# Splitting layer 0's output weights in small pieces behind the projections, and loading them ready-made

## The chip, the core and the metric

The kernel runs on one core of a Trainium2 chip. Its engines are TensorE (PE, with its weight loads shown as PEld), VectorE (DVE), ScalarE (ACT) and GpSimd (POOL). SyncE (SP) issues nearly all of the DMAs, one after the other in its own queue. The metric is the time of one execution on the device, in microseconds. Each engine works through its own instructions strictly in order, and waits at the first one whose operands or buffers are not ready.

## The reference

A two-layer encoder over 1024 tokens of width 1024, with 256 memory tokens. Layer 0 projects the normalised input to three groups of heads and a gate: A (windowed attention with a bias and a sink), B (dense attention) and X (attention into the memory). Layer 1 has differential attention in place of A and B. What matters here is the end of each layer:

```python
def even_layer(x, mem_n, ...):
    h = rmsnorm(x, norm_g)
    aq, ak, av, bq, bk, bv, xq, gate = _split(h @ w_in, EVEN_SPLITS)
    ...
    y = jnp.concatenate([y_a, y_b, y_x], axis=-1) * jax.nn.silu(gate)
    return x + y @ w_out        # y: 1024 x 1024, w_out: 1024 x 1024
```

## The kernel before

Every product of the projections is made from two parts of each operand: hi, the value rounded to the type in which TensorE multiplies (fp32r), and lo, the difference. One product is three matmuls (hi·hi, hi·lo, lo·hi). So every weight that is loaded has to be split first: a cast gives hi, a subtraction gives lo.

In layer 0 the projections are *jobs*, in the order of the table JORD (`xq0 m0 g6 m1 m2 g7 m3 bk bq0 bv bq1 g3 bq2 ak av aq0 g0 aq1 g4 g1 aq2 g5 g2`: q, k, v of the heads, m0 to m3 for the memory, g0 to g7 for the gate). A job yields after each *portion* of eight matmuls (`proj_jobs`), and the attention steps pull a few portions at a time (`Jobs.pull`), so that projection matmuls stand between the matmuls of attention. When the jobs run out, at about 380 us, parts of the output projection (`pre_jobs`, tiles `pre`) take their place, until `out_proj` does the rest (tiles `po`).

An attention step makes scores (`sb`, `sa`), a softmax on ACT, DVE and POOL (`e`, `mn`, `rz`), sends the result to a second tile by a DMA (`er<-e`, a "hop"), transposes it on TensorE (`te`, `ta`), splits it (`PTh` or `PTa` on ACT, `PTl` on DVE) and multiplies it with the values (`ob`, `oa`). `ab` is the bias band of an A head, which comes from `skew_d` in DRAM. `gy` is the gated result, `yr` and `xh` are later reads.

The output weights `w_out` of layer 0 are split in `load_wout`: 16 chunks of 128 × 512, each loaded raw (`wor`), cast on ACT (`woh`), and subtracted on DVE or POOL in turn (`wol`). This can begin only when the first half of the last job (g2) has freed the tiles of the layer's input, which `wout_hook` waits for. Layer 1's weights are split in another way: the class `Early` does it in 32 pieces of 128 × 256 during the attention, keeps hi and lo in DRAM (`wo_d`), and `load_wout` loads them ready-made.

The order of the instructions on each engine is set by the framework's list scheduler, from the order in which the program is written, its dependences and hints (`tc.issue_after`). `after_fill()` is such a hint: the instruction comes after the last matmul of the projections. The weights of the projections are loaded in two halves per job by `load_w` (tile `wr`, two buffers), cast on DVE (`wh`) and subtracted on POOL, or for the jobs m0 to m3 on DVE (`wl`).

Of the kernel before, what the change touches and what calls it, by code (L numbers as in the profile page):

```python
# [155 lines left out]
def encoder_kernel(ctx, tc, A):  # L156
# [15 lines left out]
    def dma(out, in_, eng=None):  # L172
        if out.dtype == F32R and in_.dtype == F32R:
            out, in_ = out.bitcast(F32), in_.bitcast(F32)
        (eng or nc.sync).dma_start(out=out, in_=in_)  # L175
# [20 lines left out]
    for t in (spare, edge):  # L196
# [50 lines left out]


    class Early:
        def __init__(self, l, tiles):  # L250
            self.l, self.n, self.tiles, self.held = l, 0, tiles, None
# [8 lines left out]
        def step(self):  # L260
            self.store()
            if self.n < 32:
                i, c = divmod(self.n, 2)
                nh, k = divmod(i, 8)
                c = c * 256
                self.n += 1
                raw = wp.tile([P, 512], F32, tag="wr", name="wor", bufs=2)[:, 0:256]
                dma(raw, w_out[self.l][KORD[self.l][k], :, nh * 512 + c:nh * 512 + c + 256])
                hi, lo = self.tiles()
                nc.scalar.copy(hi, raw)  # L270
                nc.gpsimd.tensor_tensor(out=lo, in0=raw, in1=hi, op=ALU.subtract)
# [6 lines left out]
    def load_wout(l, i, pl):  # L278
        nh, k = divmod(i, 8)
        if k == 0:  # L280
            wtile.append([pl.tile([P, 8, 512], F32R, tag="h", name="wo" + c, bufs=4) for c in "hl"])
        hi, lo = (t[:, k, :] for t in wtile[nh])
        if l == 1:
            for t, d in zip((hi, lo), wo_d[l][nh]):
                dma(t, d[:, k, :])
            return hi, lo
        raw = sg(M, "wor", F32) if i % 2 else wp.tile([P, 512], F32, tag="wr", name="wor", bufs=2)
        dma(raw, w_out[l][KORD[l][k], :, nh * 512:(nh + 1) * 512])
        nc.scalar.copy(hi, raw)
        (nc.gpsimd if i % 2 else nc.vector).tensor_tensor(out=lo, in0=raw, in1=hi, op=ALU.subtract)  # L290
        return hi, lo

    def wout_hook(l, jobs, last, pl):
# [104 lines left out]
    def sg(M, name="sg", dt=F32R):  # L398
        return M.pl.tile([P, 512], dt, tag="sg", name=name, bufs=M.cfg["sg"])
# [311 lines left out]
    def pre_jobs(l, src):  # L711
        out = []
        for ts, k in PRE[l]:
            parts = [(0,), (1,)] if len(ts) > 1 else [(0, 1)]
            for nhs in parts:
                out.append(dict(
                    tag="pre%s%d" % (ts[0], nhs[0]), also=tuple("pre%d" % t for t in ts) if nhs[-1] else (),
                    run=lambda _, ts=ts, k=k, nhs=nhs: pre_run(l, ts, k, nhs, src), load=lambda: None,
                    when=lambda k=k, nhs=nhs: len(wout) >= 8 * nhs[-1] + 8 and all((l, m) in stored for m in range(k))))
        return out  # L720

    def pre_run(l, ts, kn, nhs, src):
# [725 lines left out]

    toeps = {}

    def halves():
        t = sg(M, "wos")
        return t[:, 0:256], t[:, 256:512]
# [202 lines left out]
```

## Time and profile before

| | us |
|---|---|
| three runs | 1240.26, 1238.16, 1237.77 |
| their median | 1238.16 |
| the profiled execution | 1240.08 |
| its span in the profile | 1238.3 |
| PE busy | 1201.8 |
| DVE busy | 793.6 |
| ACT busy | 653.7 |
| POOL busy | 429.0 |

The span runs from the first to the last recorded instruction; the profiled execution's time has 1.8 us around it. In rows of the timeline stand the start, the duration, the engine, the line, the operation, what is written and read, the shape and the count; a bracket at the end tells how long the engine was idle before it and what ended that. In rows by tile, the three numbers are the shortest, median and longest duration in ns. In rows of DMA issues, the last number is the median time in us from issue to landing. In rows of windows, the busy time of each engine stands with its number of instructions, then the clock granted to TensorE, the DMA share and GB/s. The line numbers are those of the kernel before.

### The profile page before, as it was taken

Reading aid. Unit: us, or ns where it says so; the run is one execution under the profiler, and the core shown is the slowest. Engines: PE = TensorE matmul, PEld = TensorE weight load, DVE = VectorE, ACT = ScalarE, POOL = GpSimd, SP = SyncE. Lnnn points to the kernel's source line nnn. Section 1 sums busy time; section 2 is a strip of 40 time slices with the busy share of each in tenths; the row PEclk is TensorE's granted clock in tenths of the full one; section 3 lists DMA queues with packets and bytes.
Section 4 is the critical chain, followed back from the end, with each engine's and each line's share of the span. In section 5 each row is a group of like instructions: output and inputs, shape, how many; then the busy total and the mean of one; then the engine's idle time right before and its main releaser. Section 6 shows DMA issues by size and latency. Waiting matters only on the chain.

```text
span 1238.3 us, 19903 instructions
## 1 busy us (share of the span) xinstructions
PE 1201.8 (97%) x6806; PEld 1001.2 (81%) x6806; DVE 793.6 (64%) x1471; ACT 653.7 (53%) x1469; POOL 429.0 (35%) x414
## 2 busy tenths in 40 slices
PE   6999999999999899999999999999999999999997
PEld 5788888888887778887888778788887878888886
DVE  5547665477777768637355865766666666767544
ACT  6248754367667767533157744555545454445332
POOL 5023365466666655403122222334242231201100
PEclk9999999999999989999999999999999999999999
DMA  6654445545465565466644445354453452458353
GB/s 255 199 191 146 161 170 167 167 156 203 176 229 201 195 220 197 151 200 215 191 166 147 143 154 156 136 166 156 142 175 136 149 173 95 153 205 293 124 195 145
DMA packets 112769, 216.71 MB, mean 175 GB/s; under 512 B 13303, under 2 KB 45303, under 8 KB 112669
## 3 DMA queue, kind: packets, MB, share of 16 engines
q1 hardware_dynamic: 112668, 215.45, 51.7%
q8 instruction: 54, 0.88, 0.3%
q14 instruction: 47, 0.38, 0.1%
HBM read 87.71 MB, written 39.86 MB: 103 GB/s over the span
## 4 chain that ended last, share of the span: by engine, by line
PE 51%; DVE 1%; issue 1%; DMA 0%; SPq 0%; POOL 0%; ACT 0%; POOLq 0%; DVEq 0%; ACTq 0%
PE acc L329 26%; PE oc L1530 6%; PE po L695 5%; PE sc L1491 4%; PE te L573 3%; PE sc L1497 3%; PE pre L695 2%; PE ox L649 1%; PE ssqc L1545 1%; PE tv L438 1%; PE sx L542 1%; PE rbcc L1558 0%; PE tx L377 0%; DMA wr<-in_w_mem 0%; SPq L175 0%
## 5 line engine op out<-in xcount | busy, mean ns | idle before, releaser
L329 PE MATMUL acc<-h,wh 128*128 128x512 f32 x1536 | 499.5, 399 | 1.9 <-DVE h L351 0.8
L329 PEld LDWEIGHTS acc<-h,wh 128*128 128x128 f32 x1536 | 282.6, 188 | 66.4 <-issue 12.3
L329 PE MATMUL acc<-h,wl 128*128 128x512 f32 x768 | 304.5, 396 | 1.6 <-POOL wl L243 1.6
L243 POOL TENSOR_TENSOR wl<-wr,wh 128x512 fp32r<-128x512 f32 x96 | 125.1, 1304 | 303.5 <-DVE wh L241 132.0
L348 DVE TENSOR_TENSOR PTl<-te,PTh 128x512 fp32r<-128x512 f32 x224 | 148.3, 686 | 125.3 <-ACT PTh L347 122.7
L1506 ACT ACTIVATE e<-e,mn 128x1024 f32<-128x1024 f32 x96 | 110.1, 1148 | 123.7 <-DVE mn L1503 123.7
L329 PEld LDWEIGHTS acc<-h,wl 128*128 128x128 f32 x768 | 144.6, 188 | 35.3 <-issue 4.7
L347 ACT CAST PTh<-te 128x512 fp32r<-128x512 f32 x224 | 125.1, 591 | 18.7 <-PE te L573 15.4
L1503 DVE CUSTOM_DVE_ANT_0 e<-sc,toep 128x1024 f32<-128x1024 f32 x96 | 113.9, 1217 | 7.9 <-PE sc L1497 7.8
L1107 POOL TENSOR_TENSOR e<-e,rz 128x1024 f32<-128x1024 f32 x48 | 92.4, 1929 | 76.2 <-DVE rz L1106 57.9
L573 PEld LDWEIGHTS te<-identr,er 128*128 128x128 f32 x896 | 92.2, 143 | 15.0 <-issue 3.7
L573 PE MATMUL te<-identr,er 128*128 128x128 f32 x896 | 98.7, 245 | 3.1 <-issue 2.5
L241 DVE CAST wh<-wr 128x512 fp32r<-128x512 f32 x112 | 58.7, 526 | 42.7 <-PE acc L329 17.5
L1530 PE MATMUL oc<-PTh,v 128*128 128x256 f32 x384 | 74.8, 288 | 0.7 <-DVE ckl L1406 0.7
L1515 DVE SCALAR_TENSOR_TENSOR e<-e,mr 128x1024 f32<-128x1024 f32 x48 | 66.9, 1393 | 1.4
L695 PE MATMUL po<-woh,yh 128*128 128x512 f32 (+1 forms) x172 | 65.8, 383 | 0.0
L695 PE MATMUL po<-woh,yl 128*128 128x512 f32 (+1 forms) x172 | 65.6, 381 | 0.0
L695 PE MATMUL po<-wol,yh 128*128 128x512 f32 (+1 forms) x172 | 65.5, 381 | 0.0
L1098 DVE TENSOR_REDUCE mn<-sb 128x1 f32<-128x1024 f32 x48 | 58.3, 1215 | 7.2 <-PE sb L542 6.7
L1530 PEld LDWEIGHTS oc<-PTh,v 128*128 128x128 f32 x384 | 61.4, 191 | 1.0 <-DVE ckl L1406 0.9
L350 ACT ACTIVATE yh<-yr 128x256 fp32r<-128x256 f32 (+2 forms) x56 | 24.0, 447 | 67.4 <-DMA yr<-ysc 30.6
L231 POOL TENSOR_TENSOR r<-v,nhalf 128x1 f32<-128x1 f32 (+1 forms) x28 | 19.1, 686 | 115.9 <-DVE v L1333 95.4
(201 smaller groups left out, 2303.3 us busy)
## 6 DMA issues: line engine op xcount, KB each, us to landing
er<-e SPq DMA_DIRECT2D x112, 512.0 KB, 3.1
wr<-in_w_in SPq DMA_DIRECT2D x96, 256.0 KB, 3.0
ysc<-gy SPq DMA_DIRECT2D x16, 512.0 KB, 2.8
cq<-sg SPq DMA_DIRECT2D x64, 128.0 KB, 2.6
ck<-sg SPq DMA_DIRECT2D x48, 128.0 KB, 2.3
er<-e SPq DMA_DIRECT2D x12, 384.5 KB, 2.9
xpsc<-xh SPq DMA_DIRECT2D x18, 256.0 KB, 2.6
xr<-xpsc SPq DMA_DIRECT2D x9, 512.0 KB, 4.3
```

Source lines behind the costliest of these rows:

```text
L241: nc.vector.tensor_copy(hi, raw)
L243: (nc.vector if fast else nc.gpsimd).tensor_tensor(out=lo, in0=raw, in1=hi, op=ALU.subtract)
L329: lastmm[0] = nc.tensor.matmul(acc, a, b[:, k, c0:c0 + n], start=(i == 0), stop=(i == 23))
L347: nc.scalar.copy(hi, src)
L348: return nc.vector.tensor_tensor(out=lo, in0=src, in1=hi, op=ALU.subtract)
L573: nc.tensor.transpose(to[:, i * P:(i + 1) * P], e[0][:, k * P:(k + 1) * P], idt)
L695: lastmm[0] = nc.tensor.matmul(acc, a, b, start=(start and n == 0), stop=(stop and n == 2))
L1107: nc.gpsimd.tensor_tensor(out=et, in0=et, in1=rz.to_broadcast([P, 1024]), op=ALU.mult)
L1503: nc.vector.tensor_tensor_reduce(out=et, in0=Sp, in1=toeps[h][:, w0:w0 + 1024], scale=1.0, scalar=BIG, op0=ALU.add, op1=ALU.min, accum_out ...
L1506: nc.scalar.activation(et, et, AF.Exp, bias=mn[:, m:m + 1], scale=-1.0, accum_out=z[:, m:m + 1])
L1515: nc.vector.scalar_tensor_tensor(out=es[0], in0=es[1], scalar=c, in1=es[0], op0=ALU.mult, op1=ALU.add)
L1530: nc.tensor.matmul(acc, V[:, kt, v, :], pt[:, kt, :], start=(n == 0), stop=(n == 23))
```

## The change

Layer 0 now uses `Early` too. After the job xq0, each portion of the projections calls `early.tick()` (through `Jobs.tick`). A piece takes two ticks: the first stores the piece before and loads the next; the second splits it. The tile `wos` holds both parts, [128, 2, 256], and comes from a pool of its own with one buffer. The raw piece is loaded into its second half, cast on DVE into its first half, and the subtraction on POOL replaces the raw values by lo. One store of 256 KB then puts both into DRAM. `load_wout` is left with two loads of 256 KB for each of the 16 chunks, and no arithmetic. In layer 1 the pieces go through the same code, in a tile of the pool `sg`, with the cast on ACT as before, one store in place of two, and no raw piece in the weights' buffers `wr`. A job of the output projection may start as soon as the chunks that it uses first are there.

```diff
@@ class Jobs
+        self.tick = None
@@ Jobs._advance, after a portion
+        if self.tick is not None:
+            self.tick()
         return True
@@
-    wo_d = [[[dr.tile([P, 8, 512], F32R, name="wo%d%d%s" % (l, nh, c)) for c in "hl"] for nh in range(2)]
-            for l in range(2)]
+    wo_d = [[dr.tile([P, 8, 2, 512], F32R, name="wo%d%d" % (l, nh)) for nh in range(2)] for l in range(2)]
@@ class Early
         def store(self):
             if self.held is not None:
-                hi, lo, nh, k, c = self.held
-                for d, t in zip(wo_d[self.l][nh], (hi, lo)):
-                    dma(d[:, k, c:c + 256], t)
+                t, nh, k, c = self.held
+                dma(wo_d[self.l][nh][:, k, :, c:c + 256], t)
                 self.held = None
...
+        def load(self):
             if self.n < 32:
...
-                raw = wp.tile([P, 512], F32, tag="wr", name="wor", bufs=2)[:, 0:256]
-                dma(raw, w_out[self.l][KORD[self.l][k], :, nh * 512 + c:nh * 512 + c + 256])
-                hi, lo = self.tiles()
-                nc.scalar.copy(hi, raw)
-                nc.gpsimd.tensor_tensor(out=lo, in0=raw, in1=hi, op=ALU.subtract)
-                self.held = hi, lo, nh, k, c
+                t = self.tile()
+                dma(t[:, 1, :].bitcast(F32), w_out[self.l][KORD[self.l][k], :, nh * 512 + c:nh * 512 + c + 256])
+                self.raw = t, nh, k, c
+
+        def split(self):
+            if self.raw is not None:
+                t = self.raw[0]
+                with after_fill():
+                    self.copy(t[:, 0, :], t[:, 1, :].bitcast(F32))
+                    nc.gpsimd.tensor_tensor(out=t[:, 1, :], in0=t[:, 1, :].bitcast(F32), in1=t[:, 0, :],
+                                            op=ALU.subtract)
+                self.held, self.raw = self.raw, None
+
+        def tick(self):
+            if self.raw is not None:
+                self.split()
+            else:
+                self.store()
+                self.load()
@@ load_wout
-        if l == 1:
-            for t, d in zip((hi, lo), wo_d[l][nh]):
-                dma(t, d[:, k, :])
-            return hi, lo
-        raw = sg(M, "wor", F32) if i % 2 else wp.tile([P, 512], F32, tag="wr", name="wor", bufs=2)
-        dma(raw, w_out[l][KORD[l][k], :, nh * 512:(nh + 1) * 512])
-        nc.scalar.copy(hi, raw)
-        (nc.gpsimd if i % 2 else nc.vector).tensor_tensor(out=lo, in0=raw, in1=hi, op=ALU.subtract)
+        for j, t in enumerate((hi, lo)):
+            dma(t, wo_d[l][nh][:, k, j, :])
@@ pre_jobs
-                    when=lambda k=k, nhs=nhs: len(wout) >= 8 * nhs[-1] + 8 and all(...)
+                    when=lambda k=k, nhs=nhs: len(wout) >= 8 * nhs[-1] + k and all(...)
@@ layer 0
+    stage = pool(left, "stage", "left")
+    early = Early(0, lambda: stage.tile([P, 2, 256], F32R, tag="wos", name="wos", bufs=1), nc.vector.tensor_copy)
...
     jobs.ensure("xq0")
+    jobs.tick = early.tick
@@ layer 1
-    early = Early(1, halves)
+    early = Early(1, lambda: sg(M, "wos").rearrange("p (a b) -> p a b", a=2), nc.scalar.copy)
```

What this does to the order is seen at three places. The first is SP's queue among the projections of the memory, around 58 us, before (`lamt`, `vec_d`, `skew_d` and `xkh`, `xkl` are small transfers of that part; `wr` are weights):

```order
L175 DMA wr<-in_w_mem 128x512 x2
L175 DMA lamt<-in_lam 128x256
L175 DMA vec_d<-vs 6x512
L175 DMA wr<-in_w_mem 128x512 x2
L175 DMA xkh<-sg 64x256 x2
L175 DMA xkl<-xkl 64x256
L175 DMA xkh<-sg 64x256 x2
L175 DMA xkl<-xkl 64x256
L175 DMA wr<-in_w_in 128x512 x2
L175 DMA skew_d<-vec_d 128x512
```

The same stretch after:

```order
L178 DMA vec_d<-vs 6x512
L178 DMA wr<-in_w_mem 128x512
L178 DMA wo_113<-wos 128x2x256
L178 DMA xkh<-sg 64x256 x2
L178 DMA xkl<-xkl 64x256
L178 DMA xkh<-sg 64x256 x2
L178 DMA xkl<-xkl 64x256
L178 DMA wos<-in_w_out 128x256
L178 DMA wr<-in_w_mem 128x512
L178 DMA wr<-in_w_in 128x512
L178 DMA skew_d<-vec_d 128x512
L178 DMA wo_113<-wos 128x2x256
```

The second of the two loads of memory weights has moved behind the store of a piece and the load of the next one, which writes the same buffer, and the second load of `in_w_in` has moved further down.

The second place is ACT at the start of the last attention steps, around 420 us, before (`mr`, `e,z` belong to a softmax, `yt` to the result of a step):

```order
L289 CAST woh<-wor 128x512
L1102 ACTIVATE mr<-mn,rq 128x1
L289 CAST woh<-wor 128x512
L1103 ACTIVATE e,z<-sb,mr,nrq 128x1024
L470 COPY yt<-oa 64x256
L347 CAST PTh<-te 128x4x128 x2
L289 CAST woh<-wor 128x512 x3
L1102 ACTIVATE mr<-mn,rq 128x1
L347 CAST PTh<-te 128x4x128
```

The same stretch after:

```order
L1119 ACTIVATE mr<-mn,rq 128x1
L1120 ACTIVATE e,z<-sb,mr,nrq 128x1024
L483 COPY yt<-oa 64x256
L360 CAST PTh<-te 128x4x128 x2
L1119 ACTIVATE mr<-mn,rq 128x1
L360 CAST PTh<-te 128x4x128
```

The casts of the weights are gone from between the softmax and the casts of the transposed tiles. Between the hops, SP now has the loads of ready-made chunks, twice as many as there were raw ones:

```order
L178 DMA er<-e 128x641
L178 DMA er<-e 128x1024 x2
L178 DMA woh<-wo_113 128x512
L178 DMA wol<-wo_113 128x512
L178 DMA woh<-wo_113 128x512
L178 DMA wol<-wo_113 128x512
L178 DMA er<-e 128x641
L178 DMA woh<-wo_113 128x512
```

Two to five of them stand between one hop and the next.

The third place is POOL around 437 us, before (`e<-e,rz` scales the softmax of a B step, the narrow ones that of an A step; `ab<-ab,mask` finishes the bias band of the next A head):

```order
L472 TENSOR_TENSOR gy<-yt,gy 64x256 x2
L1145 TENSOR_TENSOR ab<-ab,mask 128x384
L1107 TENSOR_TENSOR e<-e,rz 128x1024 x2
L1191 TENSOR_TENSOR e<-e,rz_5237 128x256
L1191 TENSOR_TENSOR e<-e,rz_5237 128x384
```

The same stretch after:

```order
L1124 TENSOR_TENSOR e<-e,rz 128x1024
L485 TENSOR_TENSOR gy<-yt,gy 64x256
L1124 TENSOR_TENSOR e<-e,rz 128x1024
L1208 TENSOR_TENSOR e<-e,rz_5364 128x256
L1208 TENSOR_TENSOR e<-e,rz_5364 128x384
L1162 TENSOR_TENSOR ab<-ab,mask 128x384
```

The instruction that finishes the bias band has moved behind the four scalings.

More of the change, by code (lines that the diff above doesn't have):

```diff
@@ L249, in encoder_kernel, with __init__ @@
     class Early:
-        def __init__(self, l, tiles):
-            self.l, self.n, self.tiles, self.held = l, 0, tiles, None
+        def __init__(self, l, tile, copy):
+            self.l, self.n, self.tile, self.copy = l, 0, tile, copy
+            self.raw = self.held = None
         def store(self):
             if self.held is not None:
-                hi, lo, nh, k, c = self.held
-                for d, t in zip(wo_d[self.l][nh], (hi, lo)):
-                    dma(d[:, k, c:c + 256], t)
+                t, nh, k, c = self.held
+                dma(wo_d[self.l][nh][:, k, :, c:c + 256], t)
                 self.held = None
-        def step(self):
-            self.store()
+        def load(self):
             if self.n < 32:
@@ L266, in step @@
                 self.n += 1
-                raw = wp.tile([P, 512], F32, tag="wr", name="wor", bufs=2)[:, 0:256]
-                dma(raw, w_out[self.l][KORD[self.l][k], :, nh * 512 + c:nh * 512 + c + 256])
-                hi, lo = self.tiles()
-                nc.scalar.copy(hi, raw)
-                nc.gpsimd.tensor_tensor(out=lo, in0=raw, in1=hi, op=ALU.subtract)
-                self.held = hi, lo, nh, k, c
+                t = self.tile()
[15 more added lines that the diff above has]
+                self.load()
+        def step(self):
+            self.store()
+            self.load()
+            self.split()
     def new_hT(pl):
@@ L718, in pre_jobs @@
                     run=lambda _, ts=ts, k=k, nhs=nhs: pre_run(l, ts, k, nhs, src), load=lambda: None,
-                    when=lambda k=k, nhs=nhs: len(wout) >= 8 * nhs[-1] + 8 and all((l, m) in stored for m in range(k))))
+                    when=lambda k=k, nhs=nhs: len(wout) >= 8 * nhs[-1] + k and all((l, m) in stored for m in range(k))))
         return out
@@ L1449, in encoder_kernel @@
     toeps = {}
-    def halves():
-        t = sg(M, "wos")
-        return t[:, 0:256], t[:, 256:512]
-    early = Early(1, halves)
+    early = Early(1, lambda: sg(M, "wos").rearrange("p (a b) -> p a b", a=2), nc.scalar.copy)
     def load_toep(h):
```

## The prediction, made before the run

> **What bounds the kernel now.** I read the page's first two parts, then TensorE's timeline for its idle spots, then cut the stretches behind them out as windows, then the instructions and transfers that ended each wait.
>
> From the page:
>
> ```profile
> span 1238.3 us, 19903 instructions
> PE 1201.8 (97%) x6806; PEld 1001.2 (81%) x6806; DVE 793.6 (64%) x1471; ACT 653.7 (53%) x1469; POOL 429.0 (35%) x414
> ...
> PE   6999999999999899999999999999999999999997
> PEld 5788888888887778887888778788887878888886
> ...
> PEclk9999999999999989999999999999999999999999
> ```
>
> TensorE is the bound: 97% busy, and between the ends each of the rows PE and PEclk has one digit below 9: PE the slice from 402 us, the clock the one from 433 us. So the change can win only idle time and lost clock of TensorE, and it loses whatever it makes TensorE wait. The three large waits inside the span are these, each the first matmul behind one:
>
> ```profile
> 391.36 0.51 PE L573 MATMUL te<-identr,er 128*128 128x128 f32 x4 [2.48 <-issue]
> 424.77 0.38 PE L1120 MATMUL ob<-PTh,v 128*128 128x256 f32 x1 [3.17 <-ACT PTh L347]
> 444.22 0.58 PE L1229 MATMUL oa<-PTa,av 128*128 128x256 f32 x1 [2.60 <-ACT PTa L347]
> ```
>
> Windows on the first and second, and on the stretches just behind the first and third (window, its length, busy time of PE, PEld, DVE, ACT and POOL, granted clock, DMA share, GB/s):
>
> ```profile
> 388.88:391.36 2.48, 0.00 (x1) 0.03 (x1) 2.48 (x6) 0.26 (x2) 2.07 (x2) 1.00 0.70 187
> 391.36:395.60 4.24, 4.24 (x17) 3.56 (x18) 3.71 (x8) 3.92 (x9) 2.91 (x3) 0.63 0.82 289
> 421.60:424.77 3.17, 0.00 (x1) 0.00 (x0) 0.63 (x3) 1.88 (x5) 1.26 (x1) 1.00 0.39 152
> 444.22:450.50 6.28, 6.28 (x24) 5.50 (x25) 4.15 (x9) 4.08 (x10) 0.77 (x2) 0.50 0.31 113
> ```
>
> Behind the first stall the clock was 0.63 over 4.24 us, which is 4.24 × 0.37 = 1.57 us of work lost. Behind the third it was 0.50 over 6.28 us: 3.14 us lost. Nothing follows the second. Altogether 2.48 + 1.57 + 3.17 + 2.60 + 3.14 = 12.96 us. That is all the middle has to give.
>
> What ended them, on DVE, POOL and ACT:
>
> ```profile
> 384.56 4.58 DVE L290 TENSOR_TENSOR wol<-wor,woh 128x512 fp32r<-128x512 f32 x2
> ...
> 384.19 3.80 POOL L290 TENSOR_TENSOR wol<-wor,woh 128x512 fp32r<-128x512 f32 x3
> ...
> 423.44 0.62 ACT L289 CAST woh<-wor 128x512 fp32r<-128x512 f32 x1 [1.29 <-DMA wor<-in_w_out]
> ...
> 437.33 1.01 POOL L1145 TENSOR_TENSOR ab<-ab,mask 128x384 f32<-128x384 f32 x1 [2.47 <-DMA ab<-skew_d]
> 438.31 3.74 POOL L1107 TENSOR_TENSOR e<-e,rz 128x1024 f32<-128x1024 f32 x2
> ...
> 443.20 0.19 ACT L1167 COPY e<-nsink 128x2 f32<-128x2 f32 x1 [2.38 <-DMA er<-e]
> ```
>
> The first stall is DVE held 4.58 us in two subtractions of the old split, beside POOL's three. The second is ACT waiting for a raw chunk ahead of the PTh cast that TensorE needs. The third is no part of the split: POOL waits 2.47 us for the bias band ab, and the two e·rz behind it, their transfer and ACT's copy all come late.
>
> **Part by part: the old split goes.** Its instructions (min/median/max ns, first and last start):
>
> ```profile
> L289 ACT CAST woh<-wor x16: 601/622/635, 380.5 to 426.6; 128x512 fp32r<-128x512 f32 x16
> L290 DVE TENSOR_TENSOR wol<-wor,woh x8: 672/682/3980, 381.2 to 426.0; 128x512 fp32r<-128x512 f32 x8
> L290 POOL TENSOR_TENSOR wol<-wor,woh x8: 1260/1288/1720, 384.2 to 428.4; 128x512 fp32r<-128x512 f32 x8
> ```
>
> Off ACT: 16 × 0.62 = 10.0 us. Off DVE: 8 × 0.68 = 5.5 plus 3.3 for the long one, 8.8 us. Off POOL: 8 × 1.29 = 10.3 us. None is work of TensorE; what it frees is the first two stalls, 7.22 us with the clock. In the third, the order now puts ab's addition behind two e·rz and two of the narrow ones, so the 2.47 us no longer hold up that er: up to 5.74 us.
>
> **32 loads come into the middle.** Sixteen raw loads of 256 KB become 32 of the same size, +4.2 MB, on the SP queue, some ahead of an er hop. Layer 1 does these loads already:
>
> ```profile
> woh<-wo10h SPq DMA_DIRECT2D x8, 256.0 KB, 5.4
> er<-e SPq DMA_DIRECT2D x112, 512.0 KB, 3.1
> ...
> 1090.00:1140.00 50.00, 50.00 (x284) 39.77 (x282) 36.42 (x67) 23.90 (x50) 3.69 (x5) 1.00 0.84 288
> ...
> L175 SPq DMA_DIRECT2D er<-e x6: 470/471/482, 1091.9 to 1138.5; - x6
> ...
> DMA to landing us min/median/max: 2.8/3.8/4.1
> ```
>
> The last two rows are er alone in that window: among the loads a hop lands in 3.8 us, 0.7 later than usual, and TensorE is busy for 50.00 of 50 us. But six hops in 50 us is few; here an er follows every two to five loads in SP's order. Best case: no new stall, 0. Worst: all of the 12.96 comes back. I take one new stall like the first with its clock, 2.48 + 1.57 = 4.05, since an er that must queue as long as a load lands 2.3 us later (5.4 against 3.1). Gain in the middle: 12.96 − 4.05 = 8.9 us.
>
> Here a rule speaks against the 12.96. The Trainium skill, "TensorE: Matmul & The Clock Gate", "What's actually happening", has the clock halved after an idle activity window of 3413 ns. By it, gaps of 2.48 and 2.60 us need cost no clock, and the middle would hold 8.25 us. The trace disagrees: both were followed by a lower clock, while the gap of 3.17 was not, so I keep the measured sums.
>
> **The pieces come in early.** 32 pieces, each with a load of 128 KB, a DVE cast, a POOL subtraction, a store of 256 KB. Nearest rows:
>
> ```profile
> L241 DVE CAST wh<-wr x112: 396/426/2002, 12.5 to 1077.2; 128x512 fp32r<-128x512 f32 x112
> L271 POOL TENSOR_TENSOR wos<-wor,wos x32: 730/750/1223, 695.4 to 1007.9; 128x256 fp32r<-128x256 f32 x32
> ...
> xpsc<-xh SPq DMA_DIRECT2D x18, 256.0 KB, 2.6
> ...
> wor<-in_w_out SPq DMA_DIRECT2D x32, 128.0 KB, 2.3
> ...
> 58.00:262.00 204.00, 201.54 (x1148) 172.03 (x1147) 122.98 (x214) 116.35 (x271) 88.51 (x71) 1.00 0.50 168
> ```
>
> DVE gets at most 32 × 0.43 = 13.7 us (the row is twice the width; I take 0.3, so 10), POOL 32 × 0.75 = 24 us, in a stretch where they are busy 123 and 89 of 204 us. As mere load that is hidden: POOL 113 and DVE 133 of 204. It is not hidden when one stands just ahead of something TensorE needs. The extra traffic is 32 × 384 KB = 12.6 MB in 204 us, 62 GB/s on top of 168; the DMA share goes from 0.50 to about 0.7, less than the 0.84 above.
>
> A rule worth weighing is in the Trainium skill, "SBUF — State Buffer", "Who interferes with whom": a two-input DVE operation and a GpSimd operation that reads SBUF take one port pair as an exclusive lock, and the loser fully blocks. The 4.58 us of the old split, two subtractions of 0.68, agree with it. It would let 24 us of new POOL work block DVE; by it, if a third met such an operation, 8 us more of DVE, still in idle time of DVE.
>
> The cost is more likely the single buffer. Load n+1 waits for store n to have landed, on SP, in front of weights and er hops. One cycle: 2.3 + 0.3 to 0.43 + 0.75 + 2.6 = 6.0 to 6.1 us, to which each issue and each in-order wait on DVE and POOL adds. By the rows of before at which the casts now stand in DVE's order, pieces are due from 58 to 262 us, 30 intervals of 6.8 us. So the loop just keeps pace, with 0.7 us to spare. Where it is offered faster, it holds SP. That is so first here:
>
> ```profile
> 57.70 1.39 SPq L175 DMA_DIRECT2D wr<-in_w_mem  x2
> ...
> 63.53 1.07 SPq L175 DMA_DIRECT2D wr<-in_w_in  x2
> ...
> 66.74 0.43 DVE L241 CAST wh<-wr 128x512 fp32r<-128x512 f32 x1 [0.83 <-DMA wr<-in_w_in]
> 67.78 1.08 DVE L241 CAST wh<-wr 128x512 fp32r<-128x512 f32 x1 [0.61 <-DMA wr<-in_w_in]
> ```
>
> The second half of m2's weights, issued at about 58.3, now stands behind the load of piece 3, and that behind the store of piece 2; it goes out near 64, and g7's second half stands behind a piece too. DVE already waits for these weights before (0.83 and 0.61). I get 1.5 and 0.5 us of stall. Later, the er hops have room:
>
> ```profile
> 147.35 8.55 SPq L175 DMA_DIRECT2D er<-e  x2
> ...
> 157.90 0.80 PE L573 MATMUL te<-identr,er 128*128 128x128 f32 x8
> ```
>
> The first of these lands at about 150.5, 7.4 us ahead of its transposes. I allow 2.5 us more for the denser places: 4.5 us of early cost in all. Ends: 0 if every place has such room; at a cycle of 7.4 us, 30 × 0.6 less 6 us of room, 12 us. I stay near the low end because the rows give 6.0 to 6.1. Nothing excludes a small gain, but I see no source: TensorE was idle 2.46 us of those 204.
>
> **Layer 1.** 32 stores fewer and raw pieces no longer in the weights' buffers; TensorE's digits there are 9 throughout, so 0.
>
> **Sum.** −8.9 + 4.5 = −4.4 us. The profiled execution took 1240.08 us for its span of 1238.3, against a median of 1238.16, inside the runs' 1237.77 to 1240.26. 1240.08 − 4.4 = 1235.7; its excess of 1.92 over the median lies outside the terms, so I put them on the median: 1233.8, given as 1234.0.
>
> **Rivals.** *The single buffer gates the front* (slower): each in-order wait adds to the cycle until it exceeds the offered 6.8 us, SP falls behind, weights and er hops follow. For it speak the missing slack and DVE's waits for weights; against it, the 7.4 us of room later. At 7.5 us the early cost is 30 × 0.7 − 6 = 15 us; with 8.9 gained, +6.1: 1244. Early cost equals the gain at 30 × (c − 6.8) − 6 = 8.9, c = 7.3 us. From there it decides.
>
> *The gain goes to new stalls in the middle* (same): loads ahead of er hops on every A step. Two stalls like the third with its clock, 2 × 5.74 = 11.5, leave 1.5 of the 12.96; less the early 2 us of the dense place, 1238.7. For it: 5.4 us landings and er's 2.38 us wait on ACT before; against: 50 of 50 us busy in layer 1.
>
> *All is hidden* (faster): early cost 0 to 2, no new stall, 12.96 gained: 1225.2 to 1227.2.
>
> **How the numbers follow.** A measurement here can tell about 0.2%, 2.5 us. Chances: the forecast (1229 to 1236) 0.38, buffer gating 0.28, the same 0.17, hidden 0.17. Faster takes the hidden case and the forecast's part below 1235.7, 0.36: 0.53. Slower is the gating, 0.28. The same has 0.17 and the forecast's edge of 0.02, 0.19. The range 1226 to 1247 cuts the lowest half of the hidden case (0.07) and gating above a cycle of 7.6 us (0.1). Cases of both signs are in it; the forecast's own range stands above.
>
> **What the profile after would show.** Right: no DVE wait at L290 near 385, no gap at 388.9 and 421.6, one gap of 2 to 3 us between 380 and 430 with a te behind it, a clock of 1.00 around 445, early gaps of TensorE of about 2 us near 66 and some of half a microsecond. The wos casts would stand 6.8 us apart. Wrong: casts over 7.3 us apart with wr or er ended by late SP issues (gating); several te gaps with half clock between 380 and 450 (the same); a front with 201.5 of 204 busy and none in the middle (hidden). A long stall of POOL behind a wos cast on DVE, or a gate that halves the clock in the front, is what the sum has no term for.

## The result: 1.4 to 1.7% slower

The changed kernel took 1256.47 us (median of four runs, 1256.12 to 1259.74) against 1239.21 us for the kernel before beside it; the ratio is 1.0154, with a 95% interval of 1.0138 to 1.0169. The medians are 17.3 us apart, and by the ratio it is 19 us, slower where 4.4 us faster was forecast. The profiled execution of after took 1259.74 us, its span 1258.0.

The page of after, first parts:

```profile
span 1258.0 us, 20005 instructions
PE 1209.3 (96%) x6806; PEld 1003.1 (80%) x6806; DVE 804.6 (64%) x1495; ACT 645.9 (51%) x1453; POOL 445.5 (35%) x438
...
PE   6988999989999999998999999999999999999998
PEld 5777787778888888887888777887888888788886
...
PEclk9998999999999999999999999999999999999999
```

The digits below 9 of the rows PE and PEclk, which stood at 402 and 433 us, are gone from the middle. They stand in the front now, from 62 us on, where before had none, and one of PE at 566 us, on the way into layer 1.

To see where time is lost and won, each matmul of after is paired with the same matmul of before (the k-th of those with the same names), and the difference of their starts taken: the *lag*, as a median over the matmuls of before in the 10 us from the time given (20 us in the table further down). It is 0 up to 60 us, 9.2 at 100, 19.7 at 220, 27.75 from 280 to 380, then falls to 15.3 at 450, and is 16.9 at 500, 19.3 at 640 and 19.9 at the end. So the front cost 27.75 us and the middle won 12.5.

The same stretches as windows. First 58 to 262 us of after, as the prediction shows it of before; then the middle, 375 to 455 us of before, and the stretch in which after does the same work, 402.75 to 470.3 us by the lag:

```profile
58.00:262.00 204.00, 189.40 (x1029) 157.67 (x1027) 116.79 (x209) 103.81 (x239) 98.33 (x86) 0.97 0.58 195
```

```profile
375.00:455.00 80.00, 70.38 (x416) 59.96 (x415) 59.51 (x114) 54.99 (x127) 49.97 (x43) 0.94 0.59 208
```

```profile
402.75:470.30 67.55, 65.53 (x416) 56.37 (x415) 49.83 (x106) 46.31 (x110) 37.63 (x35) 1.00 0.85 298
```

In the front TensorE ran 1029 matmuls where before ran 1148, and was busy for 189.4 of 204 us instead of 201.5. In the middle it does the same 416 matmuls in 67.55 us instead of 80, at full clock and at a DMA share of 0.85.

What holds it up is seen around 266 us. The stall on TensorE, VectorE's queue, and SP's:

```profile
268.86 0.38 PE L1137 MATMUL ob<-PTl,v 128*128 128x256 f32 x1 [2.56 <-DVE PTl L361]
```

```profile
267.86 0.29 DVE L276 CAST wos<-wos 128x256 fp32r<-128x256 f32 x1 [3.51 <-DMA wos<-in_w_out]
268.07 0.15 DVE L1123 RECIPROCAL rz<-z 128x1 f32<-128x1 f32 x1
268.14 0.67 DVE L361 TENSOR_TENSOR PTl<-te,PTh 128x512 fp32r<-128x512 f32 x1
```

```profile
260.88 0.38 SPq L178 DMA_DIRECT2D wo<-wos  x1
...
263.92 0.72 SPq L178 DMA_DIRECT2D wos<-in_w_out  x1
```

The cast of a piece stands in VectorE's queue 3.51 us with nothing to do: its load went out at 263.92, behind the store of the piece before at 260.88. The reciprocal and the PTl behind it could have run; TensorE waits 2.56 us for that PTl. At 97 us it is the same with one engine more: the cast waits 1.62 us, rz stands behind it, ScalarE waits 2.81 us for rz ahead of sq, qg, rot and PTh, and TensorE 2.87 us.

The third large stall of the front, at 202 us, came by another road:

```profile
187.34 1.90 POOL L1124 TENSOR_TENSOR e<-e,rz 128x1024 f32<-128x1024 f32 x1 [0.72 <-DVE rz L1123]
...
187.44 1.94 DVE L276 CAST wos<-wos 128x256 fp32r<-128x256 f32 x1 [0.19 <-DMA wos<-in_w_out]
...
194.59 0.43 DVE L243 CAST wh<-wr 128x512 fp32r<-128x512 f32 x1 [4.61 <-DMA wr<-in_w_in]
...
201.94 1.05 PE L842 MATMUL ssq<-small,sq 128*128 128x2 f32 x8 [2.69 <-ACT sq L829]
```

Here the cast of a piece did not wait but took 1.94 us instead of 0.29, beside a scaling on GpSimd. The subtraction came late by that, SP waited 2.8 us for it at the store, and the projections' weights behind that store went out at 191.17 only. VectorE waited 4.61 us for them, ahead of an mn; ScalarE waited 6.02 us for the mn, ahead of the sq that TensorE needs.

Over the whole front, the waits of the pieces on three engines (what waited, for what; us, times, the longest):

```profile
DVE wos L276 <- DMA wos<-in_w_out: 36.9, 17, 4.7
```

```profile
POOL wos L277 <- DVE wos L276: 53.3, 21, 8.7
POOL wos L277 <- DVE rz L1123: 18.4, 4, 5.9
```

```profile
SPq L178 <- POOL wos L277: 69.1, 30, 5.1
...
SPq L178 <- DMA wo<-wos: 11.8, 14, 2.9
```

Each engine stands at its link of the chain: VectorE at the cast for the load, GpSimd at the subtraction for the cast, SP at the store for the subtraction. What is queued behind is late on all three.

The three stalls told above also cost clock. The stretches of half clock at or behind them are the only ones of the front:

```profile
101.95:108.78 6.83, 6.45 (x19) 5.48 (x20) 3.83 (x7) 3.77 (x13) 3.65 (x3) 0.50 0.37 134
204.35:207.76 3.41, 3.41 (x9) 2.64 (x8) 3.41 (x4) 0.88 (x3) 3.41 (x2) 0.50 0.50 189
269.20:272.61 3.41, 3.41 (x18) 3.15 (x17) 1.75 (x6) 2.17 (x5) 3.41 (x4) 0.50 0.56 217
```

TensorE is busy for 13.3 us of them, so half the clock costs 6.6 us. Between 58 and 293 us it is idle for 19.4 us, against 2.5 before. So 17.0 us of the 27.75 are idle time and 6.6 are clock; the other 4 us stand in neither, and where they go is not shown.

### The profile page after: what moved, and what is told of

It reads as the page before. It is cut to its first block, busy times and chain, and to the rows that moved or that the text cites. A ratio compares the mean times of both kernels' runs of the same rounds, so it can differ in the third digit from the quotient of the medians.

```text
span 1258.0 us, 20005 instructions
## 1 busy us (share of the span) xinstructions
PE 1209.3 (96%) x6806; PEld 1003.1 (80%) x6806; DVE 804.6 (64%) x1495; ACT 645.9 (51%) x1453; POOL 445.5 (35%) x438
## 4 chain that ended last, share of the span: by engine, by line
PE 55%; DMA 2%; DVE 2%; ACT 1%; issue 1%; SPq 1%; POOL 0%; POOLq 0%; DVEq 0%; ACTq 0%
PE acc L342 24%; PE po L708 8%; PE oc L1544 5%; PE pre L708 4%; PE sc L1505 3%; PE te L586 3%; PE sc L1511 3%; PE ob L1137 1%; DMA wr<-in_w_mem 1%; PE ox L662 1%; PE ssqc L1559 1%; DMA yr<-ysc 1%; SPq L178 1%; PE tv L451 0%; PE sb L555 0%
## 5 line engine op out<-in xcount | busy, mean ns | idle before, releaser
L342 PEld LDWEIGHTS acc<-h,wh 128*128 128x128 f32 x1536 | 283.5, 189 | 67.0 <-issue 12.5
L277 POOL TENSOR_TENSOR wos<-wos 128x256 fp32r<-128x256 f32 x64 | 57.1, 894 | 125.3 <-DVE wos L276 53.3
L1529 DVE SCALAR_TENSOR_TENSOR e<-e,mr 128x1024 f32<-128x1024 f32 x48 | 73.3, 1528 | 1.3
```

Source lines behind the costliest of these rows:

```text
L342: lastmm[0] = nc.tensor.matmul(acc, a, b[:, k, c0:c0 + n], start=(i == 0), stop=(i == 23))
L1529: nc.vector.scalar_tensor_tensor(out=es[0], in0=es[1], scalar=c, in1=es[0], op0=ALU.mult, op1=ALU.add)
```

## The experiments

Each run stands beside the kernel before on the same chip, whose medians were 1237.7 to 1238.4 us (1239.21 beside after). The lag over the 20 us from each of five times of before shows where each lost or won. e1, e5, e15 and e16 leave layer 0's split out, so they are measurements and no versions.

| run | us | ratio, 95% interval | lag at 100 | 220 | 340 | 440 | 640 |
|---|---|---|---|---|---|---|---|
| after | 1256.47 | 1.0138 to 1.0169 | 10.8 | 19.7 | 27.8 | 15.3 | 19.3 |
| e1 middle alone | 1229.44 | 0.9922 to 0.9957 | -0.6 | -0.6 | -0.6 | -13.0 | -10.2 |
| e2 front alone | 1266.52 | 1.0219 to 1.0257 | 12.8 | 22.3 | 32.4 | 29.7 | 30.1 |
| e3 store early | 1259.42 | 1.0151 to 1.0192 | 11.0 | 19.5 | 26.0 | 13.3 | 15.8 |
| e4 half pace | 1252.94 | 1.0095 to 1.0153 | 4.8 | 9.4 | 20.5 | 8.2 | 11.2 |
| e5 transfers only | 1240.87 | 1.0012 to 1.0043 | 3.4 | 4.5 | 13.1 | 0.8 | 3.0 |
| e8 three ahead | 1246.65 | 1.0054 to 1.0088 | 4.4 | 5.5 | 14.4 | 1.5 | 3.3 |
| e9 two ahead | 1248.10 | 1.0054 to 1.0100 | 12.3 | 21.7 | 21.6 | 9.4 | 11.5 |
| e11 cast on GpSimd | 1251.09 | 1.0082 to 1.0115 | 4.9 | 15.1 | 20.5 | 8.4 | 11.1 |
| e12 two ahead, half pace | 1238.99 | 0.9993 to 1.0014 | 3.4 | 3.3 | 6.9 | -6.0 | -4.0 |
| e13 later | 1242.53 | 1.0031 to 1.0071 | 4.9 | 5.1 | 11.8 | -0.5 | 1.7 |
| e15 split only | 1242.00 | 1.0023 to 1.0042 | 11.2 | 11.3 | 11.4 | -1.4 | 1.0 |
| e16 small transfers | 1246.35 | 1.0044 to 1.0080 | 3.7 | 10.6 | 14.3 | 2.0 | 4.3 |
| e18 two ahead on GpSimd | 1241.61 | 1.0014 to 1.0032 | 7.8 | 8.4 | 13.8 | 1.0 | 3.5 |
| e19 half of it | 1238.97 | 0.9995 to 1.0014 | 3.3 | 3.5 | 3.7 | -4.4 | -1.0 |
| e20 half, held | 1242.56 | 1.0021 to 1.0040 | 0.0 | 0.3 | 5.2 | -2.8 | 0.2 |
| e21 all, held | 1242.08 | 1.0018 to 1.0040 | -0.9 | 0.0 | 10.0 | -0.7 | 2.0 |
| e22 second half, in the window | 1237.28 | 0.9982 to 1.0000 | -0.7 | 1.7 | 1.8 | -6.0 | 0.2 |
| e23 first half, in the window | 1236.43 | 0.9967 to 0.9986 | 0.0 | 2.4 | 2.5 | -1.7 | -1.4 |

The lags are those of one profiled execution each, so they and the medians need not agree to the last us or two (the profiled execution of e2 was 3.5 us above its median). In every run the middle wins: where there are no old splits left, 11 to 13 us between the columns 340 and 440, of which some 2 to 4 are given back by 640.

### The two parts by themselves

e1, middle alone:

```diff
-    jobs.tick = early.tick
@@ load_wout, layer 0
-            dma(t, wo_d[l][nh][:, k, j, :])
+            dma(t, bq_d[i % 6][:, 512 * j:512 * j + 512])
```

> The change without its front: no pieces are loaded, split or stored among the projections, and the 32 loads of the middle read other ready-made data of the same size in DRAM, so layer 0's split is left out altogether. My theory (the front lost about 27.7 us, the middle won about 12.5): the whole gain of the middle remains, 12 to 14 us, 1239.2 - 13 = about 1226. Rival (the 32 loads of the middle cost a stall, and the trace of after shows a gain only since the late front shifted the work): a gain of 9 us or less, 1230 or more.

Measured 8.6 us faster (1229.44 against 1238.00). That is the rival's gain of 9 us or less, but not for the rival's reason: the profile shows 12.4 us won by 440, as in after, and 2.8 lost again by 640. What takes these back is open. The window 375 to 455 us of e1, beside that of before shown above:

```profile
375.00:455.00 80.00, 77.22 (x493) 66.57 (x492) 59.60 (x126) 56.36 (x134) 44.38 (x42) 1.00 0.85 293
```

493 matmuls against 416, and the clock whole. The 32 loads made no new stall there: TensorE has no idle gap of 0.6 us or more between 380 and 430 us.

e2, front alone: `load_wout` as before for layer 0, pieces as in after.

> The pieces of the front as in after, but the middle splits raw chunks as before, so the pieces in DRAM are not read. My theory: the loss of the front alone, 27.7 us by the trace, 1265 to 1268. Rival (part of the front's loss is given back in the middle whatever is done there, because layer 0's attention has slack): under 1258.

Measured 28.5 us slower than before (1266.52). So the front loses its 28 us whatever is behind it, and the two parts add up: 28.5 - 8.6 = 19.9, against the 17 to 21 us that the interval of after gives.

### Distance and pace

e3, store early:

```diff
             if self.raw is not None:
                 self.split()
+                self.store()
             else:
-                self.store()
                 self.load()
```

> The store of a piece is issued in the portion of its split, and the load alone in the next one. The one buffer and the cycle's sum stay. Theory A (the cast stands in VectorE's order one portion of some 3.4 us behind a load that must first wait 2.6 us for the store to land and then 2.4 us for itself): the cast's data now come in time, and half or more of the front's 27.7 us goes, 1240 or less. Theory B (the whole cycle of the single buffer, with its waits, is longer than the 6.8 us offered): nothing changes, 1253 to 1259.

Measured 1259.42: nothing changed, and VectorE waited 35.3 us at 16 casts. Theory A's remedy failed; the order had put the casts at nearly the same places (33.0, 58.1, 66.9 to 289.3 us, where after has 33.0, 57.7, 66.5 to 291.2).

e4, half pace (`tick` returns at once at each second portion):

> A piece goes on at each second portion only, so four portions per piece instead of two, spread over all of the projections, with one buffer. Theories A and B both: the loop has twice the time and the front's loss goes but for 2 to 6 us, 1228 to 1233. Theory C (it is the pieces' traffic and their work on VectorE and GpSimd that cost, wherever they stand): the loss stays near 27 us, 1250 or more, or half of it at half the density, about 1242.

Measured 1252.94. Neither theory A nor B holds as I put it: with twice the portions per piece, 20.5 us of the front's loss stayed, and VectorE still waited 32.5 us at 17 casts. The stalls were of the kind shown above. The casts stood from 33 to 347 us instead of 33 to 291: not at half the density at all, so this run does not show what half the density would do.

e8, three ahead: four portions to a piece, load at the first, split and store at the last.

> Half the pace (a piece takes four portions), one buffer, and the load now stands three portions ahead of its split, with the store in the split's portion. At half the pace alone 1253 us were measured, with 32.5 us of VectorE's waiting at casts for their loads. Theory A: the distance from load to cast is what counts, the waits at the casts fall below 10 us, and the time to 1232 to 1240. Theory D (each piece costs its 0.6 us wherever it stands, because a cast and a subtraction in the queues delay a softmax that TensorE needs): 1248 to 1256.

1246.65, between the two. The waits at casts fell to 18.6 us, the front's loss to 14.4.

e9, two ahead: two raw tiles in place of one, each piece loaded before the one ahead of it is split.

> Full pace, but two buffers for the raw pieces, and each loaded one piece ahead of the one that is split (three portions ahead of its split); hi has a tile of its own and a store of its own, so 32 stores more; 560 bytes of padding in SBUF make room. Theory A (load to cast): VectorE's 36.9 us at casts fall below 10 and the time to 1232 to 1242. Theory D (work in the queues, wherever its data are): 1250 or more. A rival for the cost that is left: SP's 96 instead of 64 DMAs in the front.

1248.10. VectorE's waits for piece loads fell to 6.4 us, with 7.3 more for the store of the last hi, but the front still lost 21.6, all of it before 220 us. So the waits at the pieces' casts are not the only way. VectorE waited there also at the casts of the projections' weights, 14 times, where before it did so 6 times:

```profile
DVE wh L243 <- DMA wr<-in_w_in: 9.7, 10, 2.4
DVE wh L243 <- DMA wr<-in_w_mem: 4.3, 4, 1.9
```

In before these two waits are 6.7 us (5 times) and 0.3 us (once), in after 10.4 us (5 times) and 0.7 us (twice). So they do not explain the whole 21.6 us; the expectation's rival, 32 more DMAs on SP, was not tested by itself.

### Which part of a piece costs

e5, transfers only: each piece is loaded into both halves of its tile and stored, without cast and subtraction.

> As after, but each piece is loaded twice, into both halves of its tile, and stored, with no cast and no subtraction in the front: the split of layer 0 is left out, the transfers are all there and 128 KB more for each piece. Theory A (a cast on VectorE that waits for its load holds up the attention behind it): with nothing on VectorE and GpSimd the front costs 0 to 6 us, and with the middle's gain of 8.6 the time is 1229 to 1236. Theory C (traffic, or weights and hops held up in SP's queue): the front still costs 15 us or more, 1245 to 1258.

1240.87, so 11 to 12 us slower than e1. Theory A's bound of 6 us is broken: without any work of the pieces on VectorE and GpSimd, the front lost 13.1. It lost 8.6 of that at one place, where VectorE stood at a cast of weights:

```profile
244.52 0.43 DVE L243 CAST wh<-wr 128x512 fp32r<-128x512 f32 x1 [6.29 <-DMA wr<-in_w_in]
244.86 1.22 DVE L1118 TENSOR_REDUCE mn<-sb 128x1 f32<-128x1024 f32 x1
```

The softmax's mn stands behind that cast. It is the same mechanism with another cast. The load of these weights was issued at 237.5 us and landed 6.9 us later, where the median in before is 2.9; that the pieces' transfers made it slow is likely but not shown, since before also has two of 6.5.

e11, the cast of a piece on GpSimd: `nc.gpsimd.tensor_copy` for `nc.vector.tensor_copy`.

> As after, with the cast of each piece on GpSimd ahead of its subtraction, so VectorE never waits for a piece. Theory A in its narrow form (VectorE's softmax behind the waiting cast is what TensorE misses): the front's loss falls to 5 to 12 us, 1235 to 1243; the wait moves to GpSimd, where the scaling of the softmax (e by rz) and the weights' subtractions stand behind it. Rival (it does not matter on which queue the wait stands): 1252 to 1262.

1251.09: the rival nearly, though some 5 us better than after. GpSimd waited 75.2 us at 18 casts. That TensorE's stalls came from there is not shown: most of its longer waits ended with VectorE and ScalarE, one step further on.

e15, split only: casts and subtractions on a tile that is loaded once.

> The engines' part alone: 32 casts on VectorE and 32 subtractions on GpSimd at the full pace, on one tile that was loaded once; no piece is loaded or stored, and the middle loads other ready-made data, so the split itself is left out. The transfers alone cost 13 us of the front by the profile, all together 27.7. Theory A (what costs is the wait of a cast for its load, and the transfers that push weights back): the front costs 0 to 3 us and the time is 1228 to 1232. Theory D (the added work itself delays softmax work in the queues): the front costs 8 to 15 us, 1238 to 1245.

1242.00, but this run did not measure what it was to measure. With no load to wait for, the order drew the splits forward, up to twelve casts in a row on VectorE ahead of a gate:

```order
L277 CAST wos<-wor 128x256 x12
L476 SCALAR_TENSOR_TENSOR gy<-gy,acc 128x512
```

TensorE waited 6.92 us for that one instruction, and the lag went from 1.9 to 11.4 there. It shows something else that matters: the portion at which a piece is written does not hold it. All 32 casts stood by 77 us, so the hint of `after_fill`, which is on a matmul of the projections, did not hold VectorE's queue here. What the part ahead of the prediction says of that hint is too much.

e16, small transfers: load and store of 8 columns in place of 256, on one lasting tile.

> As after, with the same instructions in nearly the same order, but each piece's load and store move 8 columns instead of 256, on one lasting tile, and the middle loads other ready-made data: the split is left out. The 12 MB of the pieces are gone, the fixed time of a transfer, the chain load, cast, subtraction, store on one buffer and the places in the queues are all there. Theory A (in-order waits on a chain whose links have fixed times): most of the front's 27.7 us stays, the front costs 15 to 25 us, 1244 to 1255. Theory C (bandwidth: the pieces slow the weights and the hops): the front costs 0 to 6 us, 1229 to 1236.

1246.35, inside A's times, with a front a little below A's 15 us: with the bytes gone it still lost 14.3 us, and VectorE waited 24.5 us at casts. A load of a thirty-second of the bytes landed in 2.4 us (median) against 2.6 in after, a store in 1.6 against 2.2. How the other half of the loss divides between bytes and the somewhat shorter chain is not settled.

### Where pieces can stand

e12, two ahead and half the pace:

> Two raw buffers with each piece loaded one piece ahead, and half the pace: the load is six portions ahead of its split. Theory A: the waits at the casts nearly vanish and the front costs what the transfers cost at half density, 4 to 8 us: 1233 to 1238. Theory D: 14 us or more, as with three portions ahead: 1245 or more.

1238.99, level with before; the front lost 6.9 us, as theory A had it, and the time is 1 us above its range. e13, from portion 30 on at three portions to a piece:

> As the last one, but beginning only behind the projections of the memory (portion 30), with three portions for each piece. Where the first pieces stood, between 60 and 110 us, every variant lost 4 to 12 us, since weights come just in time there. Theory: that part goes, the front costs 2 to 6 us, 1231 to 1236, below the kernel before. Rival (the loss moves to the denser later portions): 1240 or more.

1242.53, the rival's time: the loss at 100 us was still 4.9, and 6.7 us more were lost between 220 and 340. e18, as e12 with the cast on GpSimd:

> Two raw buffers loaded one piece ahead and half the pace, as in the run that came out level with before at 1239.0, with the cast on GpSimd instead of VectorE. There the front's loss was 6.8 us, its three stalls each ended by VectorE, which waited 24 us at casts, most of it for the store of the last hi. Theory: with VectorE free of the pieces the front loses 2 to 4 us, 1233 to 1236, faster than before. Rival (GpSimd's e by rz behind the waiting cast delays the hops): 1239 to 1245.

1241.61, the rival: GpSimd is no better place. e19, half of the pieces from portion 36 on:

> Only the second half of the output weights (16 pieces) is split early, from portion 36 on, five portions to a piece, two raw buffers loaded ahead; the first half is split in the middle as before. Theory: the front loses 1 to 3 us, the middle keeps half or more of its 8.6 us, 4 to 7: 1232 to 1237. Rival (the middle's three stalls return whole with the eight chunks that are split there): 1239 to 1242.

1238.97: front 3.7, nearly all of it at one stall at 95 us. Its first cast stood at 33 us, though it was written at portion 36: the order draws pieces forward as far as their buffers let them. So e20 and e21 hold each load:

```diff
+                with (tc.issue_after(lastdma[0].ins) if self.hi else nullcontext()):
                   dma(...)
```

> As the run with the second half of the weights alone, but each piece's load is held behind the last DMA that the program had written before it, and the first one stands at portion 46. Without that hold the order had drawn the pieces forward to where their own chain allows, the first cast to 33 us, whatever portion they were written at. Theory: the front then loses 0.5 us or less up to 100 us (it lost 3.0 at 95 us in the run before) and 0 to 2 later, the middle keeps its 7 to 8 by the profile: 1233 to 1236, faster than before. Rival (the pieces, now later, meet the attention steps from 240 us on, where the full splits lost 3 to 7 us): 1238 to 1242.

> All 32 pieces, from portion 30 on with three portions to a piece and two raw buffers, each load held behind the last DMA written before it. Without the hold this came to 1242.5, its front losing 11.8 us. Theory: the loss before 110 us (5 us) goes and that behind 240 us stays or grows: 1236 to 1240. Rival (the hold only moves the waits into denser attention): 1243 or more.

1242.56 and 1242.08. As versions both failed, e20 much as its rival had it (5.2 us lost by 340), e21 between its expectations. But their profiles narrow the question: held, the pieces cost nothing up to 220 us. The stretch 58 to 230 us of before, of after, and of e21, which has 17 casts of pieces in it where after has 21 (from 101 us on it is 17 against 16):

```profile
58.00:230.00 172.00, 169.98 (x960) 144.63 (x959) 102.48 (x176) 99.07 (x231) 71.44 (x57) 1.00 0.49 164
```

```profile
58.00:230.00 172.00, 157.60 (x870) 131.34 (x869) 107.29 (x190) 96.62 (x226) 85.96 (x74) 0.97 0.56 192
```

```profile
58.00:230.00 172.00, 170.31 (x960) 144.42 (x959) 108.37 (x191) 99.02 (x231) 83.38 (x73) 1.00 0.64 200
```

e21 moved 200 GB/s where after moved 192, at a higher DMA share, with as much work on VectorE and nearly as much on GpSimd, and ran the 960 matmuls of before. So in this stretch neither bytes nor work as such cost anything. Nor did the waits as such: up to 230 us VectorE waited at its casts as long as in after. The first row is of after, the two others are of e21:

```profile
DVE wos L276 <- DMA wos<-in_w_out: 18.1, 9, 3.7
```

```profile
DVE woy L287 <- DMA wo<-woy: 14.7, 4, 6.0
...
DVE woy L287 <- DMA wos<-in_w_out: 3.2, 2, 2.6
```

Two differences are left. One is what stands behind a cast that waits: directly behind 8.9 us of after's 18.1 it is an rz or an mn, behind 2.9 us of e21's 17.9. The other is SP's queue, which stood 50.6 us of this stretch at stores of pieces that waited for their split in after, and 10.1 us in e21. No run separates the two. Nor is it the hold alone: between 100 and 220 us e12 and e13, with two raw buffers and no hold, lost 0.3 us or less; e21 is e13 with the hold, and what the hold took away is the 4.9 us before 100. From 240 us on, in denser attention, the held pieces cost again (10 us up to 340).

e22 and e23 put 16 pieces into that stretch and leave the rest of the split in the middle, the second half of the weights early in e22, the first in e23:

> In the run with all pieces held to their portions TensorE lost nothing against before until 220 us, with 16 pieces split by then, and 10 us behind it. So here only 16 pieces, those of the second half of the weights, from portion 30 on at two portions each, held, two raw buffers: all of them fall into that stretch. The first half is split in the middle as before. Theory: the front costs 0 to 2 us, the middle wins 4.6 to 5.0 as in the two other runs with the second half alone: 1233 to 1236. Rival (at two portions a piece the chain is dense again and costs 4 us or more): 1238 to 1242.

> The same with the first half of the weights early and the second half split in the middle. The first stall (2.48 us and its clock) came from the first half's split, the second (3.17) from the raw loads of the second half. Theory: front 0 to 2 us, and the middle wins more, 5 to 8, since the stall with a clock loss goes: 1231 to 1235. Rival (the second half's split, with the ready-made loads ahead of its raw ones, holds ScalarE at the casts): 1237 to 1242.

1237.28 and 1236.43. e22 cannot be told from before, and is 1 us above its theory. e23 is faster by 2.0 us in the medians, 0.14 to 0.33% by its interval, the one version with pieces that beats both kernels, though less than I expected: of the middle it wins some 5.6 us (its lag goes from 2.4 at 340 to -3.2 at 460), since one stall of 3.23 us (sa waiting for VectorE's mn) now stands at 406 us.

## Why the prediction was wrong

*TensorE as the bound, the middle.* Right. The three stalls went, with their clock: there is no idle gap of 0.75 us or more between 380 and 445 us, and the clock is 1.00 there. The new stall of 4.05 us that I took from er hops queued behind loads did not come. Instead 2.8 us of the gain were lost again further on. The sum of this part, 8.9, was measured as 8.6 (5.3 to 9.7 by the interval of e1), with the 4.05 in the wrong place; that the two agree so well is luck.

*The early pieces, 4.5 us.* This step failed: 27.75 us by the profile, 28.5 by e2, beyond the upper end of 12 that I gave. I priced the loop (6.0 to 6.1 us against 6.8 offered), the weights on SP and the room of the er hops, and added VectorE's and GpSimd's share as mere load, "hidden" by their idle time. The sentence "It is not hidden when one stands just ahead of something TensorE needs" had no term in the sum. In VectorE's queue 17 of 32 casts waited, 36.9 us in all, and directly behind seven of these, with 20.7 us of the waiting, stands an rz or an mn. What the runs showed in its place is not the added work or the bytes by themselves (e21) but in-order waits, at VectorE's casts and SP's stores, that hold up softmax instructions and weights: 17.0 us of idle TensorE and 6.6 us of clock. The end of the prediction named a long wait of GpSimd behind a cast and a halved clock in the front as things without a term in the sum; both came (GpSimd up to 8.7 us, 6.6 us of clock). One place was right: near 66 us TensorE waited 1.73 us for the cast of weights, where 1.5 us were forecast. The 7.4 us of room that I showed for an er at 150 us is room on another queue.

*The rival of the single buffer.* Its time, from the measured interval of casts ((291.2 - 57.7) / 30 = 7.8 us), would be 30 × 1.0 - 6 = 24 us of early cost, near what came. But the interval alone does not show the cause: casts 7.8 us apart are also what a front gives that is itself 28 us late. What it had right is that each in-order wait feeds the next engine's, and that weights come late behind SP: SP waited 69.1 us at the pieces' stores, and the stall at 202 us came that way. Its remedy was not enough: with two raw buffers at full pace (e9) 21.6 us stayed. How much of the loss goes by SP's queue and how much by VectorE's is open.

*Pieces "due from 58 to 262 us".* I read places in the order as times at which a piece is offered. The order draws pieces forward until their buffer stops them, so they meet whatever stands there (e15, e19 against e20).

*The clock.* The prediction kept the rows of before, by which gaps of 2.48 and 2.60 us cost clock, against the rule it cites. After agrees with the rows: the gaps of 2.87, 2.69 and 2.56 us were each followed by a clock between 0.50 and 0.85 in the next 3.4 us, those of 1.73 us and less in the front by 1.00. I had counted this for the gain and not for the loss, where it made 6.6 of 27.75 us.

*The lock on the port pair.* The casts kept their 294 ns in the median, so most of the loss is in waiting and not in long instructions. But three of 32 took 1936, 1710 and 824 ns, and each ended 0.15 us behind a GpSimd instruction that had begun before it, as a lock would have it. The first of them is the one that led to the stall at 202 us. The prediction kept this to idle time of VectorE, at no cost.

*Layer 1.* Right within 0.6 us (lag 19.3 at 640, 19.9 at the end). At the border of the layers, near 582 us, after had a stall of 2.90 us where before has one of 1.54; its cause is open.

## What to carry to other kernels

Work that is moved under an idle share of an engine is not hidden by that share: ask for each instruction what its own operand arrives behind, and what stands behind it in the queue. A cast whose load goes out a few us ahead of it turns a slow transfer into a stall of whatever is next, on every engine of the chain, and it costs time where that next instruction is one that TensorE waits for. Where a scheduler sets the order, a piece stands where its buffers allow and not where it was written, so hold it explicitly, load it a piece ahead, and put only as many as a stretch takes without loss; then measure the front and the back of such a change by themselves.

## What was not expected of the hardware

Idle gaps of TensorE of 2.56 to 2.87 us in after were enough for 3.41 or 6.83 us at half clock, which adds 1.7 to 3.2 us to such a stall. The length of the gap alone does not decide it: behind a gap of 1.80 us (e12) and one of 1.74 us (e21) the clock was 0.78 and 0.69 over the next 3.4 us, and behind one of 2.60 us (e11) it stayed at 1.00 (rows in this order).

```profile
98.30:101.70 3.40, 3.40 (x16) 2.96 (x17) 2.85 (x6) 0.66 (x2) 2.03 (x1) 0.78 0.87 317
```

```profile
327.56:330.96 3.40, 3.33 (x15) 2.80 (x16) 3.40 (x6) 2.28 (x4) 0.08 (x1) 0.69 0.62 231
```

```profile
253.56:256.96 3.40, 3.40 (x27) 3.29 (x28) 1.43 (x3) 2.16 (x5) 1.48 (x3) 1.00 0.64 191
```

A load of 8 columns instead of 256 landed in 2.4 us instead of 2.6, and a store in 1.6 instead of 2.2, so taking away nearly all bytes shortened the two transfers of the chain by 0.8 us only.

A cast on VectorE can last until the GpSimd instruction beside it ends. In all runs 70 casts of pieces from a tile `wos` took over 0.4 us instead of 0.29, and each of them ended 0.12 to 0.18 us behind a GpSimd instruction that had begun before it. The small rq and r of GpSimd (at most 8 elements a row) did not do this: ten casts that began beside one kept their 0.27 to 0.29 us.
